# A tile that nothing uses, made 128 bytes smaller: where the left SBUF tiles of a decoder-layer kernel begin

## The chip, the cores and the metric

The kernel runs on one core of one Trainium2 chip. The metric is device time in microseconds (us) of one execution. Besides the timed runs there is one execution recorded by the hardware profiler, from which all rows of the profile come.

## The reference

One decoder layer on a residual stream `x` of 1024 rows by 1024 columns in float32: half a SwiGLU feed-forward step, a mixer made of two attentions (a sparse one that keeps 256 keys per query, and a stick-breaking one), and a second half feed-forward step.

```python
x = x + 0.5 * swiglu(rms_norm(x, g_ffn1), w1_gate, w1_up, w1_down)      # 1024 -> 2816 -> 1024
h = rms_norm(x, g_mix)
proj = h @ w_in                     # queries, keys, values, indexer, two gates
y_a = dsa_attention(...)            # indexer scores -> top 256 -> softmax attention, 8 heads
y_b = stick_breaking_attention(...) # 8 heads, strictly causal
merged = sigmoid(gate_a) * (y_a @ w_o_a) + sigmoid(gate_b) * (y_b @ w_o_b)
x = x + merged @ w_out
x = x + 0.5 * swiglu(rms_norm(x, g_ffn2), w2_gate, w2_up, w2_down)
# swiglu(h, wg, wu, wd) = (silu(h @ wg) * (h @ wu)) @ wd
```

## The kernel before

**Matmuls.** Every large product is made of 128x512 matmuls: 512 columns of a moving operand stream past a stationary operand of 128x128 that TensorE (PE) loads first. In `nc.tensor.matmul(ps, a, b)` the second argument is the stationary operand and the third the moving one. Each float32 factor is split into a high and a low part of a rounded type (fp32r), and a product is three matmuls (high by high, high by low, low by high), so the same pattern of three lines comes back everywhere: L312 to L314 (`mm3`, projections), L529 to L531 (`times`, inside `ffn_in`) and L768 to L770 (inside `ffn_out`). Every matmul loads its own stationary operand; the trace shows the loads as PEld.

**Stages in order of time.** `ffn_in` "a" (gate and up products of the first feed-forward step, Strassen-like with seven products `pa` to `pd` per pair of row blocks), `ffn_out` "a" (its down product, tile `p`), the projections and both attentions (matmuls `psf`, `psvb`, `pska`, `psq`, `psdot`, `psz`, `psy`, `psL`, `pso` between many 128x128 transposes against `ident`: `pstT`, `pspT`), the output projections, then `ffn_in` "b" and `ffn_out` "b". In the attentions the order on each engine is laid down by a recording planner (`Weave`) at build time; in the rest by the program's text and a scheduler.

**Where tiles lie.** SBUF is handed out per partition from two ends. Pools opened with `side="right"` grow down from the top; all others grow up from the bottom, above a region that the system keeps and above the constants in pool `cst`. Nearly all tiles are multiples of 512 bytes per partition, so where the first of a side begins, modulo 512 bytes, all later ones of that side begin too. Three tiles exist only to shift these places and are never read or written:

```python
 255  ctx.enter_context(tc.tile_pool(name="edge", bufs=1, side="right")).tile([P, 8], F32, name="edger")
 273  cst.tile([P, 24], F32, name="edgel")
 274  ident = cst.tile([P, P], F32, name="ident")
 277  cst.tile([P, 48], F32, name="pad")
 278  mhalf = cst.tile([P, H], F32, name="mhalf")
```

In the built program the tiles of the right side begin at 448 modulo 512 bytes, those of the left side at 64, and `ident`, which lies below `pad`, at 224. One group on the right side differs: the ring `wM` (pool `sa`) has tiles of 4224 bytes, so that its four buffers begin at 448, 320, 192 and 64. They hold the split weights of the two small query projections: `wqih` begins at 192 and `wqil` at 448, `wuqh` at 64 and `wuql` at 320. Both are moving operands of the `psq` matmuls, whose stationary operands `cqh` and `cql` lie on the right side at 448.

**Which operands lie on which side.** The operands of the feed-forward products come from a ring over both sides, in turn:

```python
 261  def wt(name):
 262      return outer.tile([P, 1024], F32R, tag="w", name=name, bufs=4)
 842  op = in_turn((wt, 4), (lambda name: pool.tile([P, 1024], F32R, tag="r", name=name, bufs=NR), NR))
 843  raw = in_turn((rawt, 2), (lambda name: pool.tile([P, 1024], F32, tag="raw", name=name, bufs=2), 2))
```

Here `outer` is on the right side, `pool` on the left, and `NR` is 5; so `op` gives right, left, right, left, right, left, right, left, left and starts again. In `ffn_in` the stationary operands (`O[...]`, names such as `a14A` and `a14S` in the trace) come from `op`, while the moving ones (`B[...]`, names `aB`, `aT`) lie in `tpool` on the right side. In `ffn_out` both (`aT` or `aB` moving, `aS` or `aA` stationary) come from `op`. The loads from HBM that feed them (`raw`) alternate between the sides as well. In the projections the stream `h2` lies on the right side; the weights lie there too, or on the left.

Of the kernel before, what the change touches and what calls it, by code (L numbers as in the profile page):

```python
# [10 lines left out]
F32 = mybir.dt.float32  # L11
# [13 lines left out]
P = 128  # L25
# [222 lines left out]
def trunk(ctx, tc, x, positions, g_ffn1, w1_gate, w1_up, w1_down, g_mix, w_in, g_cq, w_uq_a, w_q_idx,  # L248
          g_q_a, g_k_a, w_uv_a, w_o_a, w_o_b, w_out, g_ffn2, w2_gate, w2_up, w2_down, inv_freq, out):
    nc = tc.nc  # L250
    cst = ctx.enter_context(tc.tile_pool(name="cst", bufs=1))
# [22 lines left out]
    ident = cst.tile([P, P], F32, name="ident")  # L274
    make_identity(nc, ident)

    cst.tile([P, 48], F32, name="pad")
    mhalf = cst.tile([P, H], F32, name="mhalf")
    nc.vector.memset(mhalf, -0.5)

# [2124 lines left out]
```

## Time and profile before

| | us |
|---|---|
| median of 3 runs | 2155.19 (2154.34 to 2155.8) |
| the profiled execution's own time | 2156.91 |
| its span, first to last instruction | 2155.1 |
| PE busy (10196 matmuls) | 2130.9 (99%) |
| DVE / ACT / POOL busy | 1524.2 / 1058.6 / 908.8 |
| mean granted TensorE clock | 0.997 |

Matmuls are pipelined: a row of one gives a duration (about 0.39 us for 128x512) that overlaps the next one's. What a matmul costs is the distance from its start to the start of the next, read from rows in order of time. A mean over many is the length of a stretch divided by the matmuls that start in it; a count in a table of stretches holds those that reach over an edge too, about two.

### The profile page before, as it was taken

What the parts mean: (1) busy time and instruction counts of PE and PEld (TensorE: products, weight loads), DVE (VectorE), ACT (ScalarE), POOL (GpSimd) and SP (SyncE); (2) the same over time, 40 slices, a digit from 0 to 9 for tenths busy, and PEclk for the clock granted to TensorE, in tenths of its full rate; (3) what the DMA queues carried; (4) which work ended last, traced back from release to release, by engine and by line L of the source; (5) the groups of instructions that cost most, each with busy time, mean ns of one, the idle gap of its engine ahead of it and who ended that gap; (6) DMA issues with size and microseconds to landing.
All of it is one profiled execution on the core that took longest, in us unless ns stands there. A gap on an engine that the chain in (4) does not pass through costs nothing.

```text
span 2155.1 us, 29838 instructions
## 1 busy us (share of the span) xinstructions
PE 2130.9 (99%) x10196; PEld 1768.9 (82%) x10196; DVE 1524.2 (71%) x2485; ACT 1058.6 (49%) x1990; POOL 908.8 (42%) x718
## 2 busy tenths in 40 slices
PE   8999999999999999999999999999999999999999
PEld 7788888888879988888878888788788888888887
DVE  7865766687875499888886768845755556488675
ACT  6333343334455356888887667435432322324443
POOL 5554655532346334421213233454555445542233
PEclk9999999999999999999999999999999999999999
DMA  5577777487685252576747744783133333259655
GB/s 148 147 247 212 231 212 229 149 313 264 202 222 163 73 176 103 214 212 173 187 136 230 256 132 136 256 285 126 45 123 99 102 95 126 93 185 328 214 172 186
DMA packets 298104, 387.79 MB, mean 180 GB/s; under 512 B 40144, under 2 KB 186224, under 8 KB 297952
## 3 DMA queue, kind: packets, MB, share of 16 engines
q1 hardware_dynamic: 285088, 343.90, 51.2%
q0 software_dynamic: 12864, 41.99, 5.4%
q8 instruction: 80, 1.31, 0.2%
q14 instruction: 72, 0.59, 0.1%
HBM read 264.67 MB, written 121.15 MB: 179 GB/s over the span
## 4 chain that ended last, share of the span: by engine, by line
PE 87%; DVE 6%; DMA 3%; issue 2%; ACT 1%; POOL 0%; SPq 0%; DVEq 0%; POOLq 0%; ACTq 0%
PE p L770 6%; PE p L769 6%; PE p L768 6%; PE psf L312 4%; PE psf L314 4%; PE psf L313 4%; PE pa L529 3%; PE pc L529 3%; PE pa L531 3%; PE pa L530 3%; PE pc L531 3%; PE pc L530 3%; PE pd L529 3%; PE pd L531 3%; PE pd L530 3%
## 5 line engine op out<-in xcount | busy, mean ns | idle before, releaser
L1369 ACT ACTIVATE junka<-u,cand,sig 128x896 bf16<-128x896 f32 (+3 forms) x124 | 134.6, 1086 | 5.9 <-DVE cand L1361 4.6
L1816 DVE TENSOR_TENSOR_SCAN left<-left,hidden 128x640 f32<-128x640 f32 (+3 forms) x64 | 89.7, 1424 | 3.0 <-ACT left L1810 2.7
L892 ACT ACTIVATE swh<-swr 128x512 fp32r<-128x512 f32 x48 | 30.2, 629 | 119.5 <-issue 56.6
L893 DVE TENSOR_TENSOR swr<-swr,swh 128x512 f32<-128x512 f32 x48 | 39.4, 821 | 36.6 <-ACT swh L892 36.5
L1871 DVE SCALAR_TENSOR_TENSOR pt<-pstT,pt 128x512 fp32r<-128x512 f32 (+1 forms) x96 | 51.7, 550 | 16.0 <-ACT pt L1868 15.2
L672 ACT ACTIVATE b0u<-b0u 128x512 f32<-128x512 f32 x20 | 12.7, 634 | 101.8 <-DVE b0u L552 86.0
L1868 ACT ACTIVATE pt<-pstT 128x512 fp32r<-128x512 f32 (+1 forms) x96 | 46.6, 496 | 24.5 <-PE pstT L1943 24.1
L1721 ACT ACTIVATE relu<-psdot 128x512 f32<-128x512 f32 (+1 forms) x80 | 39.9, 522 | 27.7 <-DVE u L1728 17.8
L769 PE MATMUL p<-aT,aS 128*128 128x512 f32 x132 | 51.7, 392 | 1.2 <-DVE aT L382 1.2
L769 PE MATMUL p<-bT,bS 128*128 128x512 f32 x132 | 51.6, 391 | 0.0
L770 PE MATMUL p<-aT,aS 128*128 128x512 f32 x132 | 51.1, 392 | 0.0
L770 PE MATMUL p<-bT,bS 128*128 128x512 f32 x132 | 51.1, 392 | 0.0
L1230 POOL DMA_DIRECT2D gd<-evg x32 | 18.1, 567 | 76.1 <-ACT evg L1225 70.6
L1728 DVE SCALAR_TENSOR_TENSOR u<-relu,WI,u 128x512 f32<-128x512 f32 (+1 forms) x70 | 46.1, 682 | 2.8 <-ACT relu L1721 1.8
L1943 PE MATMUL pstT<-ident,left 128*128 128x128 f32 x288 | 46.0, 273 | 1.7 <-DVE pt L1871 1.7
L768 PE MATMUL p<-bT,bS 128*128 128x512 f32 x132 | 47.3, 392 | 0.0
L768 PE MATMUL p<-aT,aS 128*128 128x512 f32 x132 | 45.2, 392 | 0.0
L1997 ACT ACTIVATE e<-e,mx 128x1024 f32<-128x1024 f32 (+7 forms) x52 | 40.2, 774 | 10.1 <-DVE mx L1988 9.3
L1943 PEld LDWEIGHTS pstT<-ident,left 128*128 128x128 f32 x288 | 35.6, 140 | 11.0 <-DVE pt L1871 2.8
L381 ACT ACTIVATE bT<-bt 128x512 fp32r<-128x512 f32 x44 | 26.6, 626 | 36.0 <-PE p L770 31.7
L1810 ACT ACTIVATE left<-psz 128x512 f32<-128x512 f32 (+2 forms) x96 | 43.0, 507 | 2.0 <-PE psz L1836 1.6
L1365 DVE TENSOR_SCALAR_CACHE_REDUCE junkv<-u,cand 128x512 uint8<-128x512 f32 (+1 forms) x62 | 41.7, 673 | 0.7
(3065 smaller groups left out, 8167.7 us busy)
## 6 DMA issues: line engine op xcount, KB each, us to landing
aw<-in_w_down_dram SPq DMA_DIRECT2D x33, 512.0 KB, 4.9
bw<-in_w_down_dram SPq DMA_DIRECT2D x33, 512.0 KB, 4.9
swr<-in_w_in_dram SPq DMA_DIRECT2D x48, 256.0 KB, 5.4
a0r<-in_w_gate_dram SPq DMA_DIRECT2D x22, 512.0 KB, 7.2
a1r<-in_w_up_dram SPq DMA_DIRECT2D x22, 512.0 KB, 6.4
b0r<-in_w_gate_dram SPq DMA_DIRECT2D x22, 512.0 KB, 4.1
b1r<-in_w_up_dram SPq DMA_DIRECT2D x22, 512.0 KB, 3.9
x<-in_x_dram SPq DMA_DIRECT2D x16, 512.0 KB, 6.2
```

What stands on the lines that cost most here:

```text
L312: nc.tensor.matmul(ps, ah, bh, start=first, stop=False)
L313: nc.tensor.matmul(ps, ah, bl, start=False, stop=False)
L314: nc.tensor.matmul(ps, al, bh, start=False, stop=last)
L529: nc.tensor.matmul(ps, a[:, c], b[k][:, HI], start=start and k == 0, stop=False, skip_group_check=True)
L530: nc.tensor.matmul(ps, a[:, c], b[k][:, LO], start=False, stop=False, skip_group_check=True)
L531: ins = nc.tensor.matmul(ps, a[:, l], b[k][:, HI], start=False, stop=k == 3, skip_group_check=True)
L768: nc.tensor.matmul(ps[q][m], S[:, h], T[:, HI], start=p == 0, stop=False)
L769: nc.tensor.matmul(ps[q][m], S[:, h], T[:, LO], start=False, stop=False)
L770: nc.tensor.matmul(ps[q][m], S[:, l], T[:, HI], start=False, stop=p == last)
L1369: nc.scalar.activation(junks[1][:, 0:(i + 1) * P], score[i], AF.Sign, scale=sig[:, b:b + 1], bias=cand.bitcast(F32)[:, b:b + 1], accum_out ...
L1816: nc.vector.tensor_tensor_scan(back, back, ones, 1.0, op0=ALU.mult, op1=ALU.max)
L1943: nc.tensor.transpose(tp[:, q * P:(q + 1) * P], A[n + q][:, j * P:(j + 1) * P], ident)
```

## The change

The unused tile `pad` has 16 float32 columns in place of 48, 64 bytes per partition in place of 192. Everything on the left side above it lies 128 bytes lower; the right side, `edgel` and `ident` stay. In the built program 1951 tiles lie 128 bytes lower and 874 lie where they were. Left tiles now begin at 448 modulo 512 bytes, as the right ones do. The program has the same instructions on each engine in the same order.

```diff
@@ -274,7 +274,7 @@
     ident = cst.tile([P, P], F32, name="ident")
     make_identity(nc, ident)
 
-    cst.tile([P, 48], F32, name="pad")
+    cst.tile([P, 16], F32, name="pad")
     mhalf = cst.tile([P, H], F32, name="mhalf")
     nc.vector.memset(mhalf, -0.5)
 
```

## The prediction

> **What bounds the kernel now.** I read the page first: which engine is busy, and what the chain that ended last is made of.
>
> ```profile
> span 2155.1 us, 29838 instructions
> PE 2130.9 (99%) x10196; PEld 1768.9 (82%) x10196; DVE 1524.2 (71%) x2485; ACT 1058.6 (49%) x1990; POOL 908.8 (42%) x718
> PE 87%; DVE 6%; DMA 3%; issue 2%; ACT 1%; POOL 0%; SPq 0%; DVEq 0%; POOLq 0%; ACTq 0%
> ```
>
> TensorE is the bound: 87% of the chain. A busy share of 99% does not say that each matmul runs at its best pace, so the question for a change that only moves addresses is the distance from one matmul's start to the next. I took it from two views. The first is the busy time of PE by stretch, with the matmuls (x) in each; these six stretches are the products of the first feed-forward step (85 to 420 gate and up, 420 to 600 down), everything between, the output projections, and the second step (1530 to 1860, 1860 to 2150).
>
> ```profile
> core 0: us, PE busy (x), PEclk, DMA share, GB/s
> 85.00:420.00 335.00, 335.00 (x1450) 1.00 0.71 214
> 420.00:600.00 180.00, 180.00 (x785) 1.00 0.72 249
> 600.00:1375.00 775.00, 763.48 (x4218) 1.00 0.57 173
> 1375.00:1475.00 100.00, 98.83 (x429) 1.00 0.76 266
> 1530.00:1860.00 330.00, 329.44 (x1423) 1.00 0.31 99
> 1860.00:2150.00 290.00, 290.00 (x1262) 1.00 0.62 210
> ```
>
> In the feed-forward stretches PE never rests, at full clock, and all matmuls are 128x512: 335.0 / 1448 = 231.4 ns each, 180.0 / 783 = 229.9, 329.44 / 1421 = 231.8, 290.0 / 1260 = 230.2.
>
> The second view is PE's instructions in order of time. Columns: start us, duration, engine, line, tiles, shape. First a product of `ffn_in` whose stationary operand `a14A` is a left tile (64 modulo 512) and whose moving one `aB` is a right tile (448); then one of `ffn_out` with both on the left.
>
> ```profile
> 201.06 0.40 PE L529 MATMUL pa<-aB,a14A 128*128 128x512 f32 x1
> ...
> 203.85 0.39 PE L529 MATMUL pb<-aT,a14S 128*128 128x512 f32 x1
> ```
>
> ```profile
> 550.09 0.39 PE L768 MATMUL p<-aB,aA 128*128 128x512 f32 x1
> ...
> 552.59 0.39 PE L770 MATMUL p<-aB,aA 128*128 128x512 f32 x1
> 552.81 1.07 PE L768 MATMUL p<-aT,aS 128*128 128x512 f32 x4
> ```
>
> Twelve matmuls take 2.79 us with the operands on different sides (232.5 ns each) and 2.72 us on one side (226.7). So 5.8 ns a matmul separate two stretches with the same shape, the same clock and no wait. What differs is either the side or the place modulo 512 bytes, and only the place is what the change alters. The `psq` matmuls of the two small query projections tell these apart: all their tiles are on the right side, and only the place of the moving tile in its ring differs. `wqih` and `wqil` begin at 192 and 448, `wuqh` and `wuql` at 64 and 320, the stationary tiles `cqh` and `cql` at 448. The rows of the tiles `wqih` and `wuqh` give the shortest, median and longest duration in ns (which ends a fixed time behind the next start, so that a slower pace shows in it), and the rows in time one group of six of each.
>
> ```profile
> L312 PE MATMUL psq<-wqih,cqh x12: 389/389/396, 733.2 to 817.4; 128*128 128x512 f32 x12
> L314 PE MATMUL psq<-wqih,cql x12: 389/389/393, 733.7 to 817.9; 128*128 128x512 f32 x12
> ```
>
> ```profile
> L312 PE MATMUL psq<-wuqh,cqh x16: 390/394/468, 777.1 to 911.1; 128*128 128x512 f32 x16
> L314 PE MATMUL psq<-wuqh,cql x16: 392/396/404, 777.6 to 911.6; 128*128 128x512 f32 x16
> ```
>
> ```profile
> 767.14 0.39 PE L312 MATMUL psq<-wqih,cqh 128*128 128x512 f32 x1
> ...
> 768.50 0.39 PE L1751 MATMUL psdot<-kih,qsi 128*128 128x512 f32 x1
> ```
>
> ```profile
> 849.61 0.39 PE L312 MATMUL psq<-wuqh,cqh 128*128 128x512 f32 x1
> ...
> 850.99 0.28 PE L1751 MATMUL psdot<-kih,qsi 128*128 128x256 f32 x1
> ```
>
> Six matmuls take 1.36 us (226.7 ns each) where the two places are equal or 256 bytes apart, and 1.38 us (230) where they are 128 bytes apart modulo 256; the medians are 5 and 7 ns longer. All of it is on one side. I read it so: the pace hangs on the distance of the two operands' places, modulo 256 or 512 bytes, and equal places are the good case. Left against right is 64 against 448 today, 128 apart modulo 256, like `wuq`.
>
> **The change part by part.** It removes, adds and moves no instruction; every engine's order is the same. It moves every left tile above `pad` from 64 to 448. Three kinds of matmul follow.
>
> *128x512 with operands of different places.* Going through the built program's matmuls with their addresses gives some 3500 that have a moving operand at another place than their own stationary operand or than the next one's: 854 of the 1448 in 85 to 420, 275 of 783, 841 of 1421, 548 of 1260, 205 of the 427 in 1375 to 1475. After the change all of these are 448 against 448. I price the whole stretch by the settled pace of equal places, 226.7 ns, and not the unequal ones alone: a stretch that runs from one kind into the other and back has unsettled matmuls of both kinds today, and with no change of places left all should settle. So each stretch gains its PE time less its count times 0.2267:
>
> - 85 to 420: 335.0 - 1448 x 0.2267 = 335.0 - 328.3 = 6.7 us
> - 420 to 600: 180.0 - 177.5 = 2.5 us
> - 1375 to 1475: 98.8 - 96.8 = 2.0 us
> - 1530 to 1860: 329.4 - 322.1 = 7.3 us, of which I keep 0.5 for waits at the stretch's start that count as busy
> - 1860 to 2150: 290.0 - 285.6 = 4.4 us
>
> That is 22.4 us. Nothing covers it: PE is the bound in each of these stretches and idles in none (329.44 of 330 at worst). What is late next is the feeding of PE, and the waits of PE tell how near it is:
>
> ```profile
> PE pst L443 <- DVE ay L429: 3.5, 3, 2.0
> PE psL L2035 <- DVE mx L1988: 2.3, 3, 1.8
> ...
> PE pscqt L1541 <- DMA cqn<-cqd: 1.3, 1, 1.3
> PE p L769 <- DVE aT L382: 1.2, 1, 1.2
> ```
>
> The down products have one wait for an operand (1.2 us, DVE's `aT`), and none of PE's waits names a load of the feed-forward; a PE that is 2% faster leaves that wait perhaps a few tenths longer. I take 0.4 us off.
>
> *The openings of both steps and the attentions.* Outside those stretches some 360 matmuls of the openings and of 600 to 653 are of unequal places: 360 x 5.8 ns = 2.1 us. In 653 to 1375 there are 444, of which 48 are the `wuq` ones, on the right side, which stay as they are; 396 x 5.8 = 2.3 us. There PE runs between waits for DVE and ACT (11.5 us idle in the row 600 to 1375), and a gain ahead of such a wait is lost. I take half, 1.1 us; the ends are 0 and 2.3.
>
> *Transposes and narrow matmuls.* `ident` stays at 224, and the tiles that are turned move from 64 to 448 on the left. Two groups of ten transposes of `e`, the first from a left tile, the second from a right tile (already 448):
>
> ```profile
> 1200.87 1.25 PE L2123 MATMUL pspT<-ident,e 128*128 128x128 f32 x10
> 1223.72 1.25 PE L2123 MATMUL pspT<-ident,e 128*128 128x128 f32 x10
> ```
>
> 1.25 us both, so 0. For matmuls of 256 columns I have no pair that differs in place alone; about 210 have unequal places. Bounds: minus 210 x 5.8 ns = 1.2 us if they behave like the wide ones, and plus as much if the other way round. I take 0, since each is a sum too small to matter.
>
> *The other engines.* DVE, ACT and POOL touch the moved tiles too, and loads land in them. None of these is on PE's path in the feed-forward. Their price is bounded by what the right side, at 448 all along, does with the same lines: no row tells the sides apart, and PE waits for neither. I take 0 and keep the case as a rival.
>
> Sum: 22.4 - 0.4 + 2.1 + 1.1 = 25.2 us, less about a microsecond for matmuls that stay unsettled behind transposes, a guess: 24 us. Against the span of 2155.1 that is 2131; the profiled execution took 2156.91, 1.7 above the median 2155.19 of the timed runs, and the span happens to equal that median, so the forecast for the timed median is 2131 us.
>
> **The rivals.**
>
> *The change does nothing.* If the 5.8 ns came from something that goes with the side (the distance between the tiles, the half of the memory, the ring that a tile comes from), nothing that the change does would touch it, and the time is 2155. Against it stand the `psq` rows, where the side is the same and the pace differs; but they are 28 matmuls of each line, and 20 ns in six. 8 in 100. The Trainium skill, page "SBUF — State Buffer", section "Who interferes with whom", gives PE two independent read ports, one for the moving operand and one for the weight load, and says that PE never waits on anyone. By that rule the places of the two operands can't matter, and the first term above is 0 in place of 22.4 us; the trace does not agree, with 2.79 against 2.72 us for twelve.
>
> *Only the unequal pairs gain.* If equal-place neighbours keep today's mean and only the unequal ones drop to it, the gain is smaller. Their mean: over 85 to 420 the excess over 226.7 is 6.7 us for 1448; if the 854 unequal ones carry 4.9 of it (5.8 ns each) and only that goes, the stretches give 4.9 + 1.6 + 1.2 + 4.9 + 3.2 = 15.8 us (854, 275, 205, 841, 548 times 5.8 ns), and with 1 us elsewhere 2138. 12 in 100.
>
> *Slower: the loads.* In 85 to 420, 420 to 600 and 1375 to 1475 the DMA engines are busy 0.71, 0.72 and 0.76 of the time. If transfers into left tiles at 448 (or out of them) took longer than at 64, the queue becomes the bound from 1 / 0.71 = 1.4 times today's time on. At 1.5 times, 335 x (0.71 x 1.5 - 1) = 22 us, 180 x 0.08 = 14 and 100 x 0.14 = 14, 50 us in all, against the 24 gained: 2181. Against it: `raw` fills right and left tiles in turn, so half of these loads land at 448 today, and no row of PE's waits names a load of the feed-forward. 4 in 100. The Trainium skill, page "DMA: Bandwidth & Descriptors", section "How a descriptor splits into AXI transactions", says that a transaction begins at a multiple of 256 bytes and that bytes ahead of a descriptor's start are fetched all the same. By that rule a piece of 512 bytes takes 18 beats from a place 64 past such a multiple and 22 from 192 past it, an estimate of 1.22 times from that page, under the 1.4 at which the queue would decide; no row here shows it.
>
> *The clock.* The granted clock is at full speed but for a few microseconds; a busier PE could be granted less. A drop of the mean from 0.997 to 0.99 costs 15 us, and leaves 2146. Nothing in the rows speaks for it: the stretches in which PE never rests are granted 1.00. 3 in 100.
>
> **How the numbers follow.** My forecast, 2131, has 73 in 100; its own range is 2126 (nearly all of the excess, 2.3 in the attentions, 1.2 from narrow matmuls) to 2136. The range for 8 in 10 reaches up to the second rival and a little below the first end: 2124 to 2140. About 0.2%, 4 us, is what a measurement can tell from no change. Faster by more: 73 + 12 + 3 of the clock's case, 0.88. Within 0.2%: 0.08, the first rival. Slower: 0.04.
>
> **What the profile after would show.** Right: the same counts of matmuls in the feed-forward in less time (1448 in about 328 us, 1260 in about 286); product `pa` at `a14A` in 2.72 us for twelve; `psq` with `wuqh` still at 1.38 us for six, since its tiles don't move; PE waits and the clock as before. Wrong: `pa` at 2.79 again (the side counts, not the place), or a new wait of PE for `aS`, `aA` or a load (the feed is too slow for the faster pace), or settled runs that are no longer 226.7.

## The result, and the profile after

| | before | after |
|---|---|---|
| timed runs, median (us) | 2154.77 (2152.81 to 2155.8) | 2129.43 (2125.9 to 2132.06) |
| ratio, 95% interval | | 0.9882 (0.9864 to 0.9901) |
| profiled execution, its own time (us) | 2156.91 | 2127.6 |
| its span (us) | 2155.1 | 2125.8 |

The kernel is 25.3 us faster, 1.2%; 2131 was forecast. The page of the changed kernel, the lines that answer to the first ones shown:

```profile
span 2125.8 us, 29838 instructions
PE 2105.6 (99%) x10196; PEld 1766.6 (83%) x10196; DVE 1519.8 (71%) x2485; ACT 1056.7 (50%) x1990; POOL 910.6 (43%) x718
PE 90%; DVE 3%; DMA 3%; issue 2%; ACT 1%; POOL 0%; SPq 0%; DVEq 0%; ACTq 0%; POOLq 0%
```

TensorE is as busy as before by share and does the same 10196 matmuls in 25 us less. To see where, I cut both executions at the same points of the program: the first matmul of `ffn_out` "a", of `psq`, of `psob`, of the opening of step "b", and of `ffn_out` "b". Columns: stretch, its length, PE busy with its matmuls, granted clock, DMA share, GB/s. Before:

```profile
core 0: us, PE busy (x), PEclk, DMA share, GB/s
0.00:453.70 453.70, 447.45 (x1963) 0.99 0.67 203
453.70:733.20 279.50, 277.04 (x1468) 1.00 0.64 206
733.20:1235.40 502.20, 495.96 (x2652) 1.00 0.60 182
1235.40:1502.80 267.40, 263.38 (x1304) 0.99 0.56 188
1502.80:1938.60 435.80, 434.66 (x1894) 1.00 0.34 109
1938.60:2155.10 216.50, 212.44 (x925) 1.00 0.66 225
```

After:

```profile
0.00:442.10 442.10, 438.10 (x1963) 1.00 0.68 207
442.10:718.50 276.40, 274.41 (x1467) 1.00 0.66 210
718.50:1219.50 501.00, 495.75 (x2653) 1.00 0.60 182
1219.50:1485.30 265.80, 261.43 (x1302) 0.99 0.57 189
1485.30:1912.10 426.80, 426.23 (x1893) 1.00 0.35 112
1912.10:2125.80 213.70, 209.64 (x925) 1.00 0.69 228
```

Stage by stage that is 11.6 + 3.1 + 1.2 + 1.6 + 9.0 + 2.8 = 29.3 us. The two `ffn_in` stages, where just over half of the stationary operands lay at another place than the moving ones, give most; the 500 us of the attentions from `psq` on give 1.2. Part of the first 11.6 is not the change: in the first 40 us of the profiled execution before, the granted clock was 0.91, and 1.00 after.

```profile
0.00:40.00 40.00, 34.55 (x181) 0.91 0.68 198
```

```profile
0.00:40.00 40.00, 36.44 (x193) 1.00 0.68 198
```

The matmul that starts at 40 us before starts 2.9 us earlier in the kernel after. In a kernel of the experiments below that has the gain too (both sides at 64) and the same 0.91 in its first 40 us, it starts 0.9 us earlier; so about 2 us are due to how these two executions began, by this estimate. The 4 us by which 29.3 exceeds the 25.3 between the medians are the spread of executions: the profiled one before took 2.1 us more than its median, the one after 1.8 us less. Clocks differ between executions of one kernel, and one execution below, granted 0.75 throughout (2621.8 us), is left out of its kernel's median.

The product that the prediction showed, twelve matmuls of `pa` with `a14A` on the left and `aB` on the right, in the changed kernel (rows in time; the second row is the start of the next product):

```profile
194.61 0.39 PE L529 MATMUL pa<-aB,a14A 128*128 128x512 f32 x1
...
197.33 0.39 PE L529 MATMUL pb<-aT,a14S 128*128 128x512 f32 x1
```

2.72 us in place of 2.79: 226.7 ns a matmul, the settled pace that the prediction read where both operands lay at one place. In the whole stretch 85 to 420 us it is the same:

```profile
85.00:420.00 335.00, 335.00 (x1480) 1.00 0.71 217
```

335.0 / 1478 = 226.7 ns. No distance between two starts in it is over 228 ns: there is no unsettled matmul left.

### The profile page after: what moved, and what is told of

Its sections match the earlier page's. It is cut to its first block, busy times and chain, and to the rows that moved or that the text cites. A ratio compares the mean times of both kernels' runs of the same rounds, so it can differ in the third digit from the quotient of the medians.

```text
span 2125.8 us, 29838 instructions
## 1 busy us (share of the span) xinstructions
PE 2105.6 (99%) x10196; PEld 1766.6 (83%) x10196; DVE 1519.8 (71%) x2485; ACT 1056.7 (50%) x1990; POOL 910.6 (43%) x718
## 4 chain that ended last, share of the span: by engine, by line
PE 90%; DVE 3%; DMA 3%; issue 2%; ACT 1%; POOL 0%; SPq 0%; DVEq 0%; ACTq 0%; POOLq 0%
PE p L769 6%; PE p L770 6%; PE p L768 6%; PE psf L312 4%; PE psf L313 4%; PE psf L314 4%; PE pd L530 4%; PE pd L531 3%; PE pd L529 3%; PE pa L530 3%; PE pc L529 3%; PE pa L531 3%; PE pa L529 3%; PE pc L530 3%; PE pc L531 3%
## 5 line engine op out<-in xcount | busy, mean ns | idle before, releaser
L893 DVE TENSOR_TENSOR swr<-swr,swh 128x512 f32<-128x512 f32 x48 | 44.8, 932 | 39.4 <-ACT swh L892 36.5
```

## The experiments

Three theories were open for why the change works. A: the pace hangs on the distance of the two operands' places modulo 256 bytes. B: modulo 512. C: the place 448 itself is a good one, or something else of the left side. Nearly all edits are to the unused tiles (one makes the tiles of a ring longer), so that no kernel leaves out any work. Each ratio is to runs of the kernel before on the same chip. The stretch 85 to 420 us, full of wide matmuls, is the gauge: 1448 matmuls start in it before (x1450), 1478 after (x1480).

**256 bytes apart** (left at 192, right at 448; as everywhere below, the diff is against the changed kernel):

```diff
-    cst.tile([P, 16], F32, name="pad")
+    cst.tile([P, 80], F32, name="pad")
```

> Left tiles begin at 192 modulo 512 bytes, right ones stay at 448: 256 apart. Theory A (the pace hangs on the distance of the two operands' places modulo 256 bytes): as after the change, 226.7 ns a matmul in the feed-forward, about 2130 us. Theory B (modulo 512): 256 apart is a bad distance, about 232 ns, about 2155 us. Theory C (the place 448 itself is the good one, whatever the distance): left tiles are off it again, about 2155 us.

Measured: 2128.35 us, ratio to the kernel before 0.9882 (0.9865 to 0.9898). The gauge:

```profile
85.00:420.00 335.00, 335.00 (x1480) 1.00 0.72 217
```

The same pace as after the change. B falls, and so does C as a place: the left side is at 192 here.

**Equal places, but at 64** (the left side where it was before the change, the right side moved by a larger `edger`):

```diff
-    ctx.enter_context(tc.tile_pool(name="edge", bufs=1, side="right")).tile([P, 8], F32, name="edger")
+    ctx.enter_context(tc.tile_pool(name="edge", bufs=1, side="right")).tile([P, 104], F32, name="edger")
...
-    cst.tile([P, 16], F32, name="pad")
+    cst.tile([P, 48], F32, name="pad")
```

> Left tiles at 64 as before the change; the right ones moved to 64 too, by a larger unused tile at the top. Theories A and B (distance counts): equal places, about 2130 us, twelve matmuls of pa on a14A in 2.72 us. Theory C (448 is the good place): nothing lies at 448 any more, 2155 us or worse.

Measured: 2129.64 us, 0.9892 (0.9875 to 0.991), and

```profile
85.00:420.00 335.00, 335.00 (x1480) 1.00 0.72 217
```

Here `pad` has its old size, and the gain is there all the same. What counts is where the sides lie to each other, not where the left one lies.

**32 and 64 bytes apart** (left at 480, and at 0):

```diff
-    cst.tile([P, 16], F32, name="pad")
+    cst.tile([P, 24], F32, name="pad")      # 480; [P, 32] for 0
```

> Left tiles at 480, 32 bytes from the right ones at 448. If only an equal place is good: 2155 us. If what counts is a line of 64 bytes or more that both share (480 and 448 lie in one such line): about 2130 us. If the cost grows with the distance: a little above 2130, some 2136 us.

> Left tiles at 0 modulo 512 bytes, 64 from the right ones at 448. If only equal places (or 256 apart) are good: 2155 us. If the cost grows with the distance up to 128: half of it, about 2142 us. If a line of 64 bytes counts: the next line, 2155 us.

Measured: 2153.93 us, 1.0001 (0.9992 to 1.0011), and 2155.18 us, 1.0007 (0.9997 to 1.0016). The whole gain is gone in both, and neither a cost that grows with the distance nor a shared line of 64 bytes fits. The gauge, 32 bytes first:

```profile
85.00:420.00 335.00, 335.00 (x1454) 1.00 0.72 215
```

```profile
85.00:420.00 335.00, 335.00 (x1450) 1.00 0.70 214
```

And the product `pa` with `a14A` at 32 bytes:

```profile
199.87 0.39 PE L529 MATMUL pa<-aB,a14A 128*128 128x512 f32 x1
...
202.66 0.40 PE L529 MATMUL pb<-aT,a14S 128*128 128x512 f32 x1
```

2.79 us for twelve, as at 128 bytes. So for these wide matmuls 32, 64 and 128 bytes cost alike, and 0 and 256 nothing.

**What is left: `ident`, the ring `wM`, the absolute place.** In 600 to 1375 us the wide matmuls of the changed kernel still take about 6.5 us more than 226.7 ns each would (distances between starts of 0.3 us and more, waits for the most part, are left out). The next kernels look for that, beside a repeat of the changed kernel.

> The changed kernel once more, beside the next three on one chip: ratio 0.988 to the kernel before, about 2129 us. All theories.

Measured: 2128.54 us, 0.9881 (0.9863 to 0.9899).

```diff
-    cst.tile([P, 24], F32, name="edgel")
+    cst.tile([P, 80], F32, name="edgel")
...
-    cst.tile([P, 16], F32, name="pad")
+    cst.tile([P, 88], F32, name="pad")
```

> The changed kernel with ident moved from 224 to 448 too, so that the moving operand of all transposes lies at the same place as their stationary ones; left and right tiles stay at 448. Between 600 and 1375 us the wide matmuls of the changed kernel still hold 6.4 us over 226.7 ns each. Theory: they are unsettled because a transpose against ident at another place came before. Then that excess falls to 2 us or less and the time to about 2126 us. Rival: any narrower matmul or wait unsettles them, wherever ident lies; then the excess stays at 6 us and the time at 2129.

Measured: 2127.5 us, 0.9871 (0.9855 to 0.9888), which the intervals don't separate from the repeat. The excess is read from the next kernel, which holds the same edit.

```diff
-        rawM, wM = ring_of(brief, "rawM", 1), ring_of(s, "wM", 4, (P, 4 * NW), F32R)
+        rawM, wM = ring_of(brief, "rawM", 1), ring_of(s, "wM", 4, (P, 1088), F32R)
...
-            four = lambda t: t.rearrange("p (k f) -> p k f", k=4)
+            four = lambda t: t[:, 0:min(t.shape[1], 4 * NW)].rearrange("p (k f) -> p k f", k=4)
```

> As the kernel with ident at 448, and the ring wM with tiles of 4352 bytes, so that wqih and wqil begin at 448 and wuqh and wuql at 192, 256 from their stationary operands at 448. By distance modulo 256 the 48 psq matmuls of wuq fall from about 231 to 227 ns, 0.2 us in all, too little to time; by distance modulo 512 they stay at 231. The time is that of the kernel with ident at 448 alone.

Measured: 2127.97 us, 0.9879 (0.9862 to 0.9895). Two things follow from its profile. The `psq` matmuls of `wuqh`, in the changed kernel 128 bytes from their stationary operand and here 256 (shortest, median, longest duration in ns; the changed kernel first):

```profile
L312 PE MATMUL psq<-wuqh,cqh x16: 391/394/474, 762.4 to 896.4; 128*128 128x512 f32 x16
```

```profile
L312 PE MATMUL psq<-wuqh,cqh x16: 387/389/469, 763.5 to 897.3; 128*128 128x512 f32 x16
```

The median falls by 5 ns to the 389 that `wqih` showed all along. Start to start, the three groups of six `wuqh` and `wuql` matmuls from 868 us on, which stand behind wide matmuls, take 1.39 us each in the changed kernel and 1.36 here. That is theory A once more, in tiles that the first experiments never moved against each other. And the excess of the wide matmuls in 600 to 1375, 6.45 us in the repeat by the starts in the trace, is 6.34 us here, with `ident` at 448. The theory about `ident` was mine, and it falls. Wide matmuls behind a narrower one settle within about ten steps whether `ident` is at 224 or at 448: behind 256 columns, six `psq` matmuls of `wqih` follow one another at 233, 236, 228, 233, 231 and 226 ns in the changed kernel (from 718.55 us), and at 234, 236, 228, 232, 231 and 227 here (from 719.68 us).

Last, everything at a multiple of 256 bytes (left and right at 0, `ident` at 256):

```diff
-    ctx.enter_context(tc.tile_pool(name="edge", bufs=1, side="right")).tile([P, 8], F32, name="edger")
+    ctx.enter_context(tc.tile_pool(name="edge", bufs=1, side="right")).tile([P, 120], F32, name="edger")
...
-    cst.tile([P, 24], F32, name="edgel")
+    cst.tile([P, 32], F32, name="edgel")
...
-    cst.tile([P, 16], F32, name="pad")
+    cst.tile([P, 24], F32, name="pad")
```

> Left and right tiles all begin at 0 modulo 512 bytes and ident at 256. By distance alone this is the kernel with ident at 448: the same time. If the place counts for transfers too (a piece of 512 bytes from or to a multiple of 256), the DMA share falls from 0.58 in 600 to 1375 us, and waits for loads there get shorter: 2 to 5 us less. If it counts for DVE, ACT or POOL, their mean durations change by line.

Measured: 2130.05 us, 0.9882 (0.9868 to 0.9897): no gain over the other good kernels. In 600 to 1375, the changed kernel first:

```profile
600.00:1375.00 775.00, 764.99 (x4231) 1.00 0.58 176
```

```profile
600.00:1375.00 775.00, 765.09 (x4240) 1.00 0.56 176
```

The DMA share falls from 0.58 to 0.56, in the expected direction, but the time does not follow. DVE, ACT and POOL are busy 1523.0, 1057.4 and 912.3 us, against 1519.8, 1056.7 and 910.6 in the changed kernel: the place doesn't make them faster either. Of the kernels with a good distance none is told apart from the changed one by its interval, so there is no better version to offer.

## Why the prediction was right

*The first term, wide matmuls of different places.* It was to give 22.4 us by pricing whole stretches at 226.7 ns. Both programs have the same matmuls in the same order, so what a stretch gained can be read as the change in time between the same two matmuls:

| stretch (us, before) | forecast gain (us) | measured gain (us) |
|---|---|---|
| 85 to 420 | 6.7 | 6.8 |
| 420 to 600 | 2.5 | 2.4 |
| 1375 to 1475 | 2.0 | 0.6 |
| 1530 to 1860 | 6.8 | 7.1 |
| 1860 to 2150 | 4.4 | 4.4 |
| together | 22.4 | 21.4 |

In the four stretches of the feed-forward the mechanism holds in its size too. The choice that mattered was to price the neighbours of a change of places too. By the addresses in the built program, the matmuls of unequal places gained 17.1 of the 21.4 us and their neighbours of equal places 4.3. The rival in which only the unequal pairs gain ended at 2138, and the neighbours' 4.3 us is what it leaves out.

*The step that failed: 1375 to 1475.* The prediction says that PE idles in none of these stretches. Its own row of this one has 98.83 us busy of 100, and it doesn't show the row of PE's waits that explains it, the first below; two rows of the changed kernel follow:

```profile
PE psm L314 <- POOL woa4l L301: 1.2, 1, 1.2
```

```profile
PE psm L314 <- POOL woa4l L301: 1.3, 1, 1.3
PE psm L312 <- ACT woa4h L299: 0.3, 1, 0.3
```

`woa4h` and `woa4l` are made from `woa4r`, which comes from HBM, and that load is on the chain that ended last (from 1373.23 us, for 7.11 us, in the changed kernel). The load begins 15.5 us earlier than in the kernel before, but PE stands 16.4 us earlier by then, and waits for `woa4h` too. The pace itself settled as forecast: distances between starts of under 0.3 us held 1.4 us over 226.7 ns each in this stretch before, and 0.03 after. The other 0.6 of the 2.0 us sat in a few longer distances beside waits and a narrow matmul, which stay; and the new wait, with longer distances around it, took back 0.8. In four other profiles with a good distance the stretch gained -0.4, 1.1, 1.3 and 1.5 us. In the fifth, 256 bytes apart, PE waited 2.0 us for `woa4h`, the granted clock was 0.66 from 1385 to 1395 us, and the stretch is 4.0 us longer than before.

*The openings and the attentions.* For the attentions 1.1 us were taken with the ends 0 and 2.3; from 653 to 1375 the same matmuls gained 2.1 us, and 1.8 to 4.3 in the other five profiles. Half was too low, and the upper end no bound. For the openings and 600 to 653, 2.1 us were taken, and 5.8 measured, of which the start of these two executions is about 2. That too little here and too much in 1375 to 1475 nearly cancel is luck.

*Narrow matmuls and transposes, taken as 0.* The bound was 1.2 us either way. The pairs that the trace of before did not have exist now: `wcq0h` was 128 bytes from `mhi` modulo 256 and is at the same place now. Before, then after:

```profile
L312 PE MATMUL pscq<-wcq0h,mhi x32: 274/282/368, 670.9 to 691.3; 128*128 128x256 f32 x32
```

```profile
L312 PE MATMUL pscq<-wcq0h,mhi x32: 278/283/364, 656.4 to 676.8; 128*128 128x256 f32 x32
```

No gain at 256 columns between 128 bytes apart and equal places; 0 was right. At 32 bytes apart these matmuls are even a little faster:

```profile
L312 PE MATMUL pscq<-wcq0h,mhi x32: 278/280/366, 668.5 to 688.5; 128*128 128x256 f32 x32
```

From start to start the `pscq` matmuls take 116.8 ns there, 117.9 at 64 bytes apart, and 119.8 at 0, 128 and 256 (means of 187).

*The feed as the next thing late.* 0.4 us was taken off for the wait for `aT`. The row went from 1.2 to 0.9 us, and no wait for a load of the feed-forward came:

```profile
PE p L769 <- DVE aT L382: 0.9, 1, 0.9
```

*The reading of the `psq` rows.* The two groups of six that the prediction sets side by side are not alike: the one at 849.61 us stands behind matmuls of 256 columns, the one at 767.14 behind wide ones. Behind 256 columns a group of `wqih` takes 1.39 us as well (first pair of rows). The right partner is a group of `wuqh` behind wide matmuls, which also takes 1.39 (second pair), against 1.36. So the conclusion was right, but the pair of groups shown for it mixed two causes.

```profile
733.19 0.40 PE L312 MATMUL psq<-wqih,cqh 128*128 128x512 f32 x1
...
734.58 0.28 PE L312 MATMUL psvb<-wvb00h,mhi 128*128 128x256 f32 x1
```

```profile
898.32 0.40 PE L312 MATMUL psq<-wuqh,cqh 128*128 128x512 f32 x1
...
899.71 0.39 PE L312 MATMUL psf<-mhi,wqk5203h 128*128 128x512 f32 x1
```

Against 24 us forecast stand 25.3 between medians; runs of one kernel spread by more than the difference of 1.3, so it proves no single term. The microsecond taken off for matmuls that stay unsettled behind transposes was a guess with no row behind it: such matmuls were unsettled before as well (8.0 us of excess in 600 to 1375 before, 6.5 after).

*The rivals.* That the change does nothing, by two independent read ports of which neither waits (the Trainium skill, page "SBUF — State Buffer", section "Who interferes with whom"): the runs don't agree, with 1.2% of the time from the distance of two operands' places alone. Slower loads: no sign; by stage the DMA share rose from 0.67 to 0.68 and from 0.64 to 0.66, with the same bytes in less time. The load that PE waits for in 1375 to 1475 took 7.1 us, against 7.4 before, and 6.5 to 8.4 in the other profiles at full clock, with no order by place. The clock: a mean of 0.998, against 0.997.

## What to carry to other kernels

Where TensorE is the bound, read the distance from one matmul's start to the next in steady stretches and compare it among operands from different pools: a share of 99% busy hid 2% of pace here. Let moving and stationary operands of wide matmuls begin at equal places modulo 256 bytes; an unused tile of a few bytes on one side does it, and odd sizes anywhere below shift all that follows. Price such a change by the settled pace of a whole stretch, and only where PE never waits: read the waits of each stretch by itself, since a faster PE meets a late load sooner.

## What the runs showed of the hardware that was not expected

- With the operands' places 0 or 256 bytes apart modulo 512, a 128x512 fp32r matmul follows the last at 226.7 ns; at 32, 64 and 128 bytes apart at 232 to 233 (twelve in 2.72 against 2.79 to 2.80 us). The cost does not grow with the distance. Other distances were not run.
- Matmuls of 256 columns (282 against 283 ns) and transposes (ten in 1.25 us from either side) don't show it; at 32 and 64 bytes apart those of 256 columns are 3 and 2 ns faster, not slower.
- Wide matmuls settle at 226.7 ns within about ten steps behind a narrower one, wherever `ident` lies, and in about seven behind a change from unequal to equal places (the mean of 142 such changes in the kernel before).
- Open: whether the moving operand meets the stationary one that is in the array or the next one that is being loaded. In all steady stretches here both lie at the same place, and a kernel that parts them was not run. Where a settled run of equal places gives way to unequal ones, the start of the last equal matmul lies 231.7 ns ahead of the next start at 128 bytes apart (mean of 144 such places), and 226.0 at 64; so the traces don't settle it. Why 256 bytes, no run here shows.
